# The tiles that TensorE streams begin at other addresses of SBUF; the weights' addresses keep their remainder

## The chip, the cores and the metric

The kernel runs on one core of one Trainium2 chip. The metric is device time in microseconds of one execution, here the median of several. One such execution was also profiled, and all rows below come from it.

SBUF is addressed by partition and by byte within the partition. Each of the 128 partitions holds the same layout, so a tile has one start address, counted in bytes within a partition. This case is about that number, and mostly about its remainder after division by 512.

## The reference

An encoder of two layers on 256 tokens of width 1024, in float32:

```python
for l in range(DEPTH):                      # DEPTH = 2
    x = x + 0.5 * swiglu_ffn(rms_norm(x, norm_w[l, 0]), ffn_w_in[l, 0], ffn_w_out[l, 0])
    h = rms_norm(x, norm_w[l, 1])
    j = l // 2
    if l % 2 == 0:
        x = x + attn_conv_mixer(h, ...)     # differential attention beside a 31-tap convolution
    else:
        x = x + gated_deltanet_mixer(h, ...) # a delta rule in both directions
    x = x + 0.5 * swiglu_ffn(rms_norm(x, norm_w[l, 2]), ffn_w_in[l, 1], ffn_w_out[l, 1])
return rms_norm(x, final_norm_w)

def swiglu_ffn(h, w_in, w_out):             # w_in: 1024 x 5632, w_out: 2816 x 1024
    gate, up = jnp.split(h @ w_in, 2, axis=-1)
    return (jax.nn.silu(gate) * up) @ w_out
```

So there are four feed-forward blocks (FFN 1 to 4), and between them the attention mixer (behind FFN 1) and the delta mixer (behind FFN 3).

## The kernel before, in words

**Matrix products.** x is kept transposed, features on partitions and 256 tokens along the free dimension. Almost every matrix product is made by `column`: one 128 x 128 block of weights is loaded into TensorE and 256 tokens stream past it. Both sides are split into two float32r parts (`hi` and `lo` of the weights, `xh` and `xl` of the normed x, `hh` and `hl` of the hidden layer, `ch` and `cl` of the attention mixer's output, `oo` of the delta mixer's), and each block costs three products:

```python
nc.tensor.matmul(out, hi, xh[:, k, :], start=start and k == ks[0], stop=False)
nc.tensor.matmul(out, hi, xl[:, k, :], start=False, stop=False)
nc.tensor.matmul(out, lo, xh[:, k, :], start=False, stop=stop and k == ks[-1])
```

These are lines 99 to 101 for `xh`, `xl` and for `hh`, `hl` (an FFN's second product), lines 743 to 747 for `ch`, `cl` and lines 1294 to 1296 for `oo`. Every product has a weight load of its own (PEld in the profile), which runs beside the product ahead of it. The tile that is written second in a profile's row (`hi` or `lo` in `acc<-xh,hi`) is the weights, the first one is what streams. A few products go the other way (`rows`, lines 126 to 128): there `xh` and `xl` are the weights, and 512 columns of `hi` or `lo` stream.

**Weights.** `split_next` reads sixteen-block rows of an array half a row (eight blocks, 512 KB) at a time by a DMA of the SP queue into `raw`; ScalarE writes the rounded `hi`, VectorE or GpSimd the rest `lo`. There are up to six sets of these three tiles, three that live through the whole program and three more of most phases.

**Order.** Every engine's order is that of the code, which calls generators of side work (`tick`) between the products. An FFN is 22 calls of `pair` (48 products each) with the gate's work on VectorE, ScalarE and GpSimd behind them, and then eight calls of `column` over the 22 tiles of `hh` (66 products each).

**Addresses.** Pools of tiles lie one behind another in the order in which they are opened, and tiles within a pool of single tiles in the order in which they are made; nothing in the code names an address. The constant pool starts at byte 16512 of a partition, and `normw` (192 bytes), `x` (8192), `ident` (512), `mhalf` (64), `ones` (512), `xh` and `xl` (8192 each) follow. That puts `xh` at 25984 = 50 x 512 + 384. The steps within `xh`, `hh`, `ch` and `oo` are 1024 bytes (one k tile of 256 tokens), and those within `hi` and `lo` 512 bytes (one block), so that all slices of a tile have the remainder of its start.

Of the kernel before, what the change touches and what calls it, by code (L numbers as in the profile page):

```python
# [27 lines left out]

def halves(w, on_pool=()):
    """The weights eight blocks at a time, and whether GpSimd splits them."""  # L30
    n = 2 * w.shape[0]
    return [(w[i // 2, :, i % 2 * 8 : i % 2 * 8 + 8, :], i in on_pool) for i in range(n)]


def plan(g, *srcs):
    """Order in which the weights of a phase are read: (array, split on Pool, parts)."""
    g.plan = [(*s, 1)[:3] for s in srcs]
    g.ready, g.left = [], []


def split_next(g):
    """Read 128 x 128 blocks of weights and split them into two float32r parts."""
# [30 lines left out]
def tick(g):  # L73
    """Advance the work that runs beside the projections."""
    for task in list(g.tasks):
        task[2] += task[1]
        while task[2] >= 1:
            task[2] -= 1
            if next(task[0], g) is g:
                g.tasks.remove(task)  # L80
                break
# [11 lines left out]
def column(g, out, ks, xh, xl, start=True, stop=True):  # L93
    """out[feature, token] += weights^T x over the k tiles of one feature tile."""
# [9 lines left out]
def pair(g, xh, xl):  # L104
    """Two feature tiles of a projection of the width of the model."""
# [7 lines left out]
def rows(g, banks, k0, xh, xl):  # L113
    """banks[t][token, feature] += x^T weights over four k tiles and 512 features."""
# [29 lines left out]
class Norm:  # L144
    """The factor of a root mean square norm, by token as a column and along every row."""
# [7 lines left out]
    def operand(self, f, scale=None):  # L153
        """The two parts of feature tile f of x, weighted."""
# [23 lines left out]
    def rest(self):  # L178
        """Sum over the features, power, and the diagonal matrix that spreads it."""
# [35 lines left out]
def close(g, st, f, acc, scale):  # L215
    """x += scale * acc in feature tile f, and what the next norm needs of it."""
# [12 lines left out]
def ffn(g, wi, wo, st, wcol, aside=iter(())):  # L229
    nc, tc = g.nc, g.tc  # L230
    with tc.tile_pool(name="ffn", bufs=1) as fp, tc.tile_pool(name="ffn2", bufs=2) as f2:
        hh = fp.tile([P, KF, T], F32R, name="hh")
# [43 lines left out]
def start(ctx, tc, a):  # L276
# [10 lines left out]
    nc.sync.dma_start(g.normw, a["norm_w"])  # L287
    g.x = g.const.tile([P, KD, T], F32, name="x")
    g.ident = g.const.tile([P, P], F32, name="ident")
    g.mhalf = g.const.tile([P, 16], F32, name="mhalf")  # L290
    nc.gpsimd.memset(g.mhalf, -0.5)
    g.ones = g.const.tile([P, P], F32, name="ones")
    nc.gpsimd.memset(g.ones, 1.0)
    g.xh = g.const.tile([P, KD, T], F32R, name="xh")
    g.xl = g.const.tile([P, KD, T], F32R, name="xl")
# [22 lines left out]
def first_pair(g, src, pool):  # L318
    """The first two feature tiles, k tile by k tile as x and the weights arrive."""
# [32 lines left out]
def finish(g, a, st):  # L352
    """The last norm: its factor spread over the rows, times the weighted x."""
# [12 lines left out]
def weight_pools(g, es, n):  # L366
    """Room for n more tiles of weights."""
# [3 lines left out]
def phase(g, es, n, **psum):  # L371
    """Weight buffers and PSUM banks of one phase."""
# [12 lines left out]
def ac_consts(g, a, c):  # L385
    """Constants of the mixer, a step at a time: loads, products, and the table of biases."""
# [47 lines left out]
def conv_pair(g, c, n, uT, y, others):  # L434
    """Taps n and up of the depthwise convolution for two channel tiles, one step at a time."""
# [23 lines left out]
def conv_pool(g, ap, c, n, uT, y):  # L459
    """The first n taps with products on ScalarE and sums on GpSimd."""  # L460
# [21 lines left out]
def head(g, ap, h, qT, kz, v, ch, cl, held=False):  # L482
    """One head of the attention in four steps."""
# [84 lines left out]
def staggered(gens):  # L568
    """Each generator starts one slot after the one before it."""
# [10 lines left out]
def conv_norm(g, ap, y, room, ch, cl):  # L580
    """Layer norm over the channels and silu; room holds as much as y."""
# [31 lines left out]
def attn_conv(g, a, st, wcol):  # L613
    nc, tc = g.nc, g.tc
    win, wo = a["ac_in"], a["ac_out"]
    with tc.tile_pool(name="acm", bufs=1) as mp, tc.tile_pool(name="ac2", bufs=g.nt) as ap:
        ch = mp.tile([P, 16, T], F32R, name="ch")
        cl = mp.tile([P, 16, T], F32R, name="cl")
        uT = mp.tile([P, KD, T + 2 * HC], F32, name="uT")
        y = mp.tile([P, KD, T], F32, name="y")  # L620
# [16 lines left out]
        def conv_all():  # L637
            """Up to two pairs of channel tiles side by side."""
# [58 lines left out]
        def scores_done():  # L697
            """The products of the first four heads have been issued."""
# [105 lines left out]
def gates(g, a, c, both, st, beta, gg):  # L804
    """beta and the log decay g, [token, tile, direction and head]."""
# [44 lines left out]
def short_conv(g, acc, dst, w0, ready, sums=None):  # L850
    """Five taps over tokens of two channel tiles, then silu; dst is [channel, 2, token].

    sums takes the sums of squares over the channels and eps, [token, tile, head]."""
# [33 lines left out]
def base_inverse(g, pk, Lp, d):  # L887
    """Inverse of I + L for the 16-blocks of the diagonal, one per partition; [k, i] and [i, k]."""
# [5 lines left out]
    for s in range(1, BB):  # L894
# [4 lines left out]
        tmp = pk.tile([n, BB - 1, BB - 1], F32, tag=f"tmp{d}", name="tmp")  # L899
# [10 lines left out]
def together(*its):  # L910
    """Step by step through several generators side by side."""
# [8 lines left out]
def pace(it, n):  # L920
    """n steps of a generator for each of this one."""
# [10 lines left out]
def delta_net(g, a, st, wcol):  # L932
    nc, tc = g.nc, g.tc
    win = a["gd_in"]
    with ExitStack() as es:
# [4 lines left out]
        tp = ent(tc.tile_pool(name="gdt", bufs=1))  # L940
        big = ent(tc.tile_pool(name="gbig", bufs=9))
# [30 lines left out]
        def square(t):  # L972
            """Sixteen matrices in DRAM, [row, matrix, column]."""
            return bass.AP(t.tensor, t.offset, [[P, P], [PITCH, 16], [1, P]])

        def diagonal(t):
            """The 16-blocks on their diagonals, [matrix and block, row, column]."""
# [10 lines left out]
        def decays():  # L988
            """exp of the sums of g between two tokens, zero on the masked side; kept in qk."""
# [27 lines left out]
        def kgrams(hg):  # L1017
            """L transposed: k k^T with its decays and weights."""
# [479 lines left out]
```

## Time and profile before

| | us |
|---|---|
| median of 3 runs | 1267.43 |
| lowest and highest run | 1266.06, 1270.07 |
| span of the profiled execution, first to last instruction | 1266.3 |

The three runs' times include what lies around the span; the profiled execution has no time of its own beside its span, and lies 1.1 us below the median. TensorE's clock was granted at 0.974 of full speed on the mean.

How the profile is read: PE is TensorE's products and PEld its weight loads, which run beside them; DVE is VectorE, ACT ScalarE, POOL GpSimd. A product's row has a start that is measured and an end that is modelled; products overlap, so 280 ns of one product do not mean that 280 ns pass between two. What passes between two is the distance of their starts, here called the spacing. Where a row of a tile's view gives the first and the last start of n products of one line, and every third product is of that line, the spacing is the difference of the two divided by 3 (n - 1).

### The profile page before, as it was taken

The numbers are of one execution on the slowest core, as the hardware profiler recorded it, in microseconds if no ns is written. First come the engines' busy times: TensorE is split into PE (matmuls) and PEld (weight loads), VectorE is DVE, ScalarE is ACT, GpSimd is POOL, SyncE is SP. The second block draws the span as 40 slices with busy tenths as digits, with TensorE's granted clock in tenths as the row PEclk, the third lists the DMA queues.
The fourth block names the chain that finished last, engine by engine and source line by source line (L and its number), as shares of the span: only waits on it lengthen the run. The fifth ranks groups of instructions, "written<-read, shape, count | busy, mean of one in ns | idle before, by whom it ended". The sixth has DMA issues, their size and how long they took to land.

```text
span 1266.3 us, 23706 instructions
## 1 busy us (share of the span) xinstructions
PE 1199.8 (95%) x9592; PEld 1164.4 (92%) x9592; DVE 800.1 (63%) x1250; ACT 631.2 (50%) x976; POOL 376.5 (30%) x322
## 2 busy tenths in 40 slices
PE   7999999997899999999999999999889987999997
PEld 7999999986679999999999999889869977999996
DVE  7665663999965766655565655577964555665541
ACT  6444445658876644444444444564433334444441
POOL 1111018979913311101311101147620035211101
PEclk9999999998989999999999999999889997999998
DMA  9855656454314555555565554446460025655540
GB/s 309 267 186 185 192 192 191 158 183 148 113 42 149 167 187 187 187 188 184 178 188 187 185 184 143 142 143 189 133 193 2 1 72 162 197 186 184 188 145 34
DMA packets 75325, 204.17 MB, mean 161 GB/s; under 512 B 15912, under 2 KB 26792, under 8 KB 75088
## 3 DMA queue, kind: packets, MB, share of 16 engines
q1 hardware_dynamic: 74208, 201.93, 49.7%
q8 instruction: 75, 1.23, 0.4%
q10 hardware_dynamic: 1008, 0.74, 0.2%
q14 instruction: 34, 0.28, 0.1%
HBM read 197.12 MB, written 7.62 MB: 162 GB/s over the span
## 4 chain that ended last, share of the span: by engine, by line
PE 56%; DVE 5%; DMA 2%; ACT 1%; issue 1%; POOL 0%; SPq 0%; DVEq 0%; ACTq 0%; POOLq 0%
PE acc L99 16%; PE acc L101 16%; PE acc L100 15%; PE acc L985 6%; DVE tmp L900 1%; DVE lo L56 1%; ACT hi L55 1%; DMA raw<-in_gd_out_dram 1%; DMA raw<-in_wi_dram 1%; DVE r L862 1%; PE tr L1151 1%; DVE kq L862 1%; PE tr L1006 0%; DMA raw<-in_gd_in_dram 0%; DMA lp<-gl 0%
## 5 line engine op out<-in xcount | busy, mean ns | idle before, releaser
L55 ACT CAST hi<-raw 128x1024 fp32r<-128x1024 f32 (+1 forms) x360 | 374.6, 1043 | 478.0 <-PE acc L100 296.1
L56 DVE TENSOR_TENSOR lo<-raw,hi 128x1024 fp32r<-128x1024 f32 (+1 forms) x305 | 387.2, 1272 | 248.5 <-ACT hi L55 244.4
L99 PE MATMUL acc<-xh,hi 128*128 128x256 f32 x1840 | 518.7, 283 | 7.9 <-DVE x L218 5.0
L101 PE MATMUL acc<-xh,lo 128*128 128x256 f32 x1840 | 516.5, 281 | 2.3 <-DVE lo L56 2.3
L100 PE MATMUL acc<-xl,hi 128*128 128x256 f32 x1840 | 517.4, 281 | 0.9 <-DVE xl L161 0.9
L99 PEld LDWEIGHTS acc<-xh,hi 128*128 128x128 f32 x1840 | 347.8, 189 | 11.5 <-issue 8.3
L101 PEld LDWEIGHTS acc<-xh,lo 128*128 128x128 f32 x1840 | 348.2, 189 | 3.2 <-DVE lo L56 2.9
L100 PEld LDWEIGHTS acc<-xl,hi 128*128 128x128 f32 x1840 | 347.7, 189 | 2.3 <-DVE xl L161 1.3
L101 PE MATMUL acc<-hh,lo 128*128 128x256 f32 x704 | 197.3, 280 | 0.0
L99 PE MATMUL acc<-hh,hi 128*128 128x256 f32 x704 | 197.3, 280 | 0.0
L100 PE MATMUL acc<-hl,hi 128*128 128x256 f32 x704 | 197.3, 280 | 0.0
L251 POOL TENSOR_TENSOR s<-s,bc 128x512 f32<-128x512 f32 x44 | 78.4, 1783 | 372.4 <-ACT s L250 372.4
L56 POOL TENSOR_TENSOR lo<-raw,hi 128x1024 fp32r<-128x1024 f32 x55 | 132.2, 2411 | 73.0 <-ACT hi L55 72.7
L99 PEld LDWEIGHTS acc<-hh,hi 128*128 128x128 f32 x704 | 133.7, 190 | 0.0
L101 PEld LDWEIGHTS acc<-hh,lo 128*128 128x128 f32 x704 | 133.7, 190 | 0.0
L100 PEld LDWEIGHTS acc<-hl,hi 128*128 128x128 f32 x704 | 133.7, 190 | 0.0
L176 POOL TENSOR_TENSOR sum<-sum,sq 128x256 f32<-128x256 f32 x41 | 40.3, 983 | 216.7 <-ACT sq L172 216.1
L478 POOL TENSOR_TENSOR y<-y,tp 128x256 f32<-128x256 f32 x80 | 70.7, 910 | 9.8 <-ACT tp L475 9.5
L447 DVE SCALAR_TENSOR_TENSOR cv<-uT,convw,cv 128x256 f32<-128x256 f32 x154 | 66.3, 481 | 0.6
L242 DVE TENSOR_TENSOR h<-acc,s 128x512 f32<-128x512 f32 x44 | 30.4, 691 | 27.6 <-PE acc L101 24.2
L249 DVE TENSOR_TENSOR s<-acc,bc 128x512 f32<-128x512 f32 x44 | 30.2, 691 | 23.0 <-PE acc L101 22.6
L161 DVE SCALAR_TENSOR_TENSOR xl<-x,normw,xh 128x256 fp32r<-128x256 f32 x48 | 36.5, 778 | 12.7 <-ACT xh L160 12.7
(260 smaller groups left out, 1413.1 us busy)
## 6 DMA issues: line engine op xcount, KB each, us to landing
raw<-in_wi_dram SPq DMA_DIRECT2D x172, 512.0 KB, 4.5
raw<-in_wo_dram SPq DMA_DIRECT2D x88, 512.0 KB, 4.4
raw<-in_ac_in_dram SPq DMA_DIRECT2D x40, 512.0 KB, 4.4
raw<-in_gd_in_dram SPq DMA_DIRECT2D x32, 512.0 KB, 3.9
raw<-in_ac_out_dram SPq DMA_DIRECT2D x16, 512.0 KB, 3.8
raw<-in_gd_out_dram SPq DMA_DIRECT2D x8, 512.0 KB, 5.4
raw<-in_wi_dram SPq DMA_DIRECT2D x8, 256.0 KB, 5.1
scr<-row SPq DMA_DIRECT2D x1, 2048.0 KB, 10.6
```

Of the source, the lines that this page charges most:

```text
L55: nc.scalar.copy(hi[sl], raw[sl])
L56: eng.tensor_tensor(lo[sl], raw[sl], hi[sl].bitcast(F32), op=ALU.subtract)
L99: nc.tensor.matmul(out, hi, xh[:, k, :], start=start and k == ks[0], stop=False)
L100: nc.tensor.matmul(out, hi, xl[:, k, :], start=False, stop=False)
L101: nc.tensor.matmul(out, lo, xh[:, k, :], start=False, stop=stop and k == ks[-1])
L161: nc.vector.scalar_tensor_tensor(g.xl[:, f, :], x[:, f, :], w, g.xh[:, f, :].bitcast(F32), op0=ALU.mult, op1=ALU.subtract,)
L176: nc.gpsimd.tensor_tensor(self.sum, self.sum, sq, op=ALU.add)
L242: nc.vector.tensor_tensor(h, acc, s, op=ALU.mult)
L251: nc.gpsimd.tensor_tensor(s, s, over(st.bc), op=ALU.mult)
L447: nc.vector.scalar_tensor_tensor(y[:, ct, :] if j == CW - 1 and not n else cv[:, i, :], uT[:, ct, j : j + T], g.convw[:, ct, j : j + 1], c ...
L478: nc.gpsimd.tensor_tensor(y[:, ct, :], y[:, ct, :], tp, op=ALU.add)
L985: nc.tensor.matmul(ps[:, h, :], lhsT(h), rhs(h), start=True, stop=True)
```

## The change: what it does

The edits are unused tiles that move what comes behind them (`skip`), another order of five constants, and one tile made larger (`tmp`, from 15 x 15 to 16 x 16 values). No instruction is added or removed, and on every engine the instructions stand in the order in which they stood, but for the two memsets of `ones` and `mhalf` on GpSimd at the very start, which trade places. The start addresses become these (remainder after division by 512; counts are products in the program):

| streamed tile | products | before | after |
|---|---|---|---|
| `xh`, `xl` (FFN, mixers) | 5520 | 384 | 0 |
| `hh`, `hl` of FFN 1 | 528 | 256 | 256 |
| `hh`, `hl` of FFN 2 and 3 | 1056 | 64 | 256 |
| `hh`, `hl` of FFN 4 | 528 | 96 | 256 |
| `ch`, `cl` | 384 | 256 | 256 |
| `oo` | 192 | 416 | 256 |
| `hi`, `lo` in `rows` (512 columns) | 192 | 64 | 64 |
| float32 tiles of the delta mixer (`r2`, `F0`, `F1`, `kq`) | some 600 | 96, 416 | 256 |
| `ident`, `kz`, `y`, `v0`, `v1`, `ones` | some 300 | 192 to 384 | 0 or 256 |

The weights `hi` and `lo` have remainder 64 before and after. Where the tiles of the lower rows are themselves loaded as weights (`xh` in `rows`, `r2`, `F0`, `qT`, `both`), that remainder changes with them.

```diff
+def skip(pool, n, name):
+    if n:
+        pool.tile([P, n // 4], F32, name=name)
...
-def ffn(g, wi, wo, st, wcol, aside=iter(())):
+def ffn(g, wi, wo, st, wcol, skipped, aside=iter(())):
     nc, tc = g.nc, g.tc
     with tc.tile_pool(name="ffn", bufs=1) as fp, tc.tile_pool(name="ffn2", bufs=2) as f2:
+        skip(fp, skipped, "skip_h")
         hh = fp.tile([P, KF, T], F32R, name="hh")
...
     nc.sync.dma_start(g.normw, a["norm_w"])
+    skip(g.const, 192, "skip_x")
     g.x = g.const.tile([P, KD, T], F32, name="x")
+    g.xh = g.const.tile([P, KD, T], F32R, name="xh")
+    g.xl = g.const.tile([P, KD, T], F32R, name="xl")
     g.ident = g.const.tile([P, P], F32, name="ident")
+    g.ones = g.const.tile([P, P], F32, name="ones")
+    nc.gpsimd.memset(g.ones, 1.0)
     g.mhalf = g.const.tile([P, 16], F32, name="mhalf")
     nc.gpsimd.memset(g.mhalf, -0.5)
-    g.ones = g.const.tile([P, P], F32, name="ones")
-    nc.gpsimd.memset(g.ones, 1.0)
-    g.xh = g.const.tile([P, KD, T], F32R, name="xh")
-    g.xl = g.const.tile([P, KD, T], F32R, name="xl")
+    skip(ent(tc.tile_pool(name="skip", bufs=1)), 320, "skip_w")
     g.kept_weights = weight_pools(g, ctx, 3)
...
+        skip(mp, 64, "skip_y")
         y = mp.tile([P, KD, T], F32, name="y")
...
-        tmp = pk.tile([n, BB - 1, BB - 1], F32, tag=f"tmp{d}", name="tmp")
+        tmp = pk.tile([n, BB, BB], F32, tag=f"tmp{d}", name="tmp")
...
+        skip(tp, 160, "skip_b")
         big = ent(tc.tile_pool(name="gbig", bufs=9))
...
-        st = ffn(g, a["wi"][1], a["wo"][1], st, 3)
-        st = ffn(g, a["wi"][2], a["wo"][2], st, 4)
+        st = ffn(g, a["wi"][1], a["wo"][1], st, 3, 192)
+        st = ffn(g, a["wi"][2], a["wo"][2], st, 4, 192)
...
-        st = ffn(g, a["wi"][3], a["wo"][3], st, None)
+        st = ffn(g, a["wi"][3], a["wo"][3], st, None, 160)
```

## Rows read from the trace of the kernel before

**Rows 1.** The page: busy time by engine; clock granted to TensorE in 40 slices.

```profile
PE 1199.8 (95%) x9592; PEld 1164.4 (92%) x9592; DVE 800.1 (63%) x1250; ACT 631.2 (50%) x976; POOL 376.5 (30%) x322
...
PEclk9999999998989999999999999999889997999998
```

**Rows 2.** Groups by line: shapes, count | busy us, mean ns | idle before.

```profile
L101 PE MATMUL acc<-xh,lo 128*128 128x256 f32 x1840 | 516.5, 281 | 2.3 <-DVE lo L56 2.3
...
L126 PE MATMUL acc<-hi,xh 128*128 128x512 f32 x64 | 25.2, 407 | 0.6 <-DVE x L218 0.6
...
L985 PE MATMUL acc<-r,Lt 128*128 128x128 f32 x192 | 24.2, 284 | 0.0
```

**Rows 3.** Windows: stretch, length, busy (instructions) by engine, clock, DMA share, GB/s.

```profile
core 0: us, PE busy (x) PEld busy (x) DVE busy (x) ACT busy (x) POOL busy (x), PEclk, DMA share, GB/s
30.00:137.00 107.00, 107.00 (x911) 107.00 (x910) 66.58 (x69) 50.51 (x59) 19.41 (x11) 1.00 0.65 214
137.00:197.00 60.00, 60.00 (x531) 60.00 (x531) 35.16 (x37) 28.89 (x37) 7.11 (x7) 1.00 0.60 192
440.00:547.00 107.00, 107.00 (x910) 107.00 (x910) 66.12 (x68) 51.54 (x60) 18.86 (x11) 1.00 0.58 191
547.00:611.00 64.00, 64.00 (x536) 64.00 (x535) 34.12 (x37) 29.05 (x38) 10.31 (x8) 1.00 0.56 181
625.00:736.00 111.00, 111.00 (x944) 111.00 (x944) 69.19 (x70) 52.09 (x61) 20.04 (x11) 1.00 0.60 189
816.00:922.00 106.00, 97.77 (x747) 92.41 (x746) 85.50 (x227) 56.52 (x87) 56.21 (x29) 0.95 0.53 157
1081.00:1193.00 112.00, 112.00 (x953) 112.00 (x952) 70.36 (x71) 52.33 (x61) 20.05 (x11) 1.00 0.59 189
```

**Rows 4.** Tile hl in FFN 1 to 4: count, ns min/median/max, first and last start.

```profile
L100 PE MATMUL acc<-hl,hi x176: 276/276/279, 137.2 to 196.7; 128*128 128x256 f32 x176
...
L100 PE MATMUL acc<-hl,hi x175: 283/283/283, 547.7 to 610.4; 128*128 128x256 f32 x175
...
L100 PE MATMUL acc<-hl,hi x175: 282/283/283, 736.4 to 799.0; 128*128 128x256 f32 x175
...
L100 PE MATMUL acc<-hl,hi x175: 277/278/281, 1193.7 to 1254.6; 128*128 128x256 f32 x175
```

**Rows 5.** Tile xl, the same view, in FFN 1 and FFN 4.

```profile
L100 PE MATMUL acc<-xl,hi x255: 280/280/280, 40.0 to 129.8; 128*128 128x256 f32 x128
...
L100 PE MATMUL acc<-xl,hi x315: 279/279/279, 1081.7 to 1192.6; 128*128 128x256 f32 x158
```

**Rows 6.** Tile cl, the same view, two stretches of the attention mixer's output product.

```profile
L746 PE MATMUL acc<-cl,hi x10: 281/281/281, 404.2 to 410.2; 128*128 128x256 f32 x10
...
L746 PE MATMUL acc<-cl,hi x15: 276/276/332, 412.6 to 417.2; 128*128 128x256 f32 x15
```

**Rows 7.** Tile xl at the end of the attention mixer; tile oo in the delta mixer.

```profile
L100 PE MATMUL acc<-xl,hi x10: 276/276/281, 316.8 to 319.8; 128*128 128x256 f32 x10
...
L1295 PE MATMUL acc<-oo,hi x18: 278/283/343, 1047.1 to 1053.0; 128*128 128x256 f32 x18
```

**Rows 8.** Timeline of PE where FFN 1's second product begins: start us, length us, product.

```profile
136.94 0.28 PE L101 MATMUL acc<-xh,lo 128*128 128x256 f32 x1
137.05 0.28 PE L99 MATMUL acc<-hh,hi 128*128 128x256 f32 x1
137.17 0.28 PE L100 MATMUL acc<-hl,hi 128*128 128x256 f32 x1
137.29 0.28 PE L101 MATMUL acc<-hh,lo 128*128 128x256 f32 x1
137.40 0.28 PE L99 MATMUL acc<-hh,hi 128*128 128x256 f32 x1
137.51 0.28 PE L100 MATMUL acc<-hl,hi 128*128 128x256 f32 x1
```

**Rows 9.** Line 245 on VectorE (writes hl) in FFN 1 and FFN 2; line 900.

```profile
L245 DVE TENSOR_TENSOR hl<-h,hh x8: 683/684/686, 49.0 to 128.1; 128x512 fp32r<-128x512 f32 x8
...
L245 DVE TENSOR_TENSOR hl<-h,hh x8: 684/684/686, 459.2 to 538.3; 128x512 fp32r<-128x512 f32 x8
...
L900 DVE TENSOR_TENSOR tmp<-tt,lp x30: 157/306/2181, 884.0 to 920.5; 128x1 f32<-128x1 f32 x2, 128x4 f32<-128x4 f32 x2, 128x9 f32<-128x9 f32 x2, 128x16 f32<-128x16 f32 x2
```

More of the change, by code (lines that the diff above doesn't have):

```diff
@@ L368, in weight_pools, with phase @@
     return [es.enter_context(g.tc.tile_pool(name=m, bufs=n)) for m in WEIGHTS]
-def phase(g, es, n, **psum):
+def phase(g, es, n, skipped, **psum):
+    if skipped:
+        skip(es.enter_context(g.tc.tile_pool(name="skip", bufs=1)), skipped, "skip_w")
     g.weights = [g.kept_weights] + ([weight_pools(g, es, n)] if n else [])
@@ L616, in attn_conv @@
     with tc.tile_pool(name="acm", bufs=1) as mp, tc.tile_pool(name="ac2", bufs=g.nt) as ap:
+        skip(mp, 0, "skip_c")
         ch = mp.tile([P, 16, T], F32R, name="ch")
@@ L1365, in encoder @@
     with ExitStack() as es:
-        phase(g, es, 3, acc=3, tr=2, cv=2, sc=1)
+        phase(g, es, 3, 0, acc=3, tr=2, cv=2, sc=1)
         with tc.tile_pool(name="acc_", bufs=1) as c:
@@ L1369, in encoder @@
                 g.first, st = fp, first_norm(g, 0, fp)
-                st = ffn(g, a["wi"][0], a["wo"][0], st, 1, ac_consts(g, a, c))
+                st = ffn(g, a["wi"][0], a["wo"][0], st, 1, 0, ac_consts(g, a, c))
             g.pool_in, g.pool_out, g.conv_off = range(4, 28), (), 0
             st = attn_conv(g, a, st, 2)
-        st = ffn(g, a["wi"][1], a["wo"][1], st, 3)
-        st = ffn(g, a["wi"][2], a["wo"][2], st, 4)
+        st = ffn(g, a["wi"][1], a["wo"][1], st, 3, 192)
+        st = ffn(g, a["wi"][2], a["wo"][2], st, 4, 192)
     g.post_rate, g.gram_rate, g.dec_rate, g.nr2, g.order = 3, 4, 2, 11, "kqvz"
@@ L1377, in encoder @@
     with ExitStack() as es:
-        phase(g, es, 0, acc=5, tr=3)
+        phase(g, es, 0, 0, acc=5, tr=3)
         st = delta_net(g, a, st, 5)
     with ExitStack() as es:
-        phase(g, es, 3, acc=4, tr=2)
+        phase(g, es, 3, 0, acc=4, tr=2)
         final_weight(g, a, es.enter_context(tc.tile_pool(name="fin", bufs=1)))
-        st = ffn(g, a["wi"][3], a["wo"][3], st, None)
+        st = ffn(g, a["wi"][3], a["wo"][3], st, None, 160)
         finish(g, a, st)
```

## The prediction

> **What bounds the kernel now.** I read the page first: TensorE is busy 95% of the span and its clock is granted in full nearly everywhere [rows 1]. The windows by stage say where that is more than an average: in the long stretches of the four FFNs PE is busy for all of 107, 111 or 112 us, while VectorE is busy for some 62% and ScalarE for 47% [rows 3], and no wait is counted there. In these stretches the time is the number of products times the distance between two starts. So I looked for that spacing by operand, with the tile view of a third of the products at a time.
>
> The reader is to see four numbers. The first FFN's second product runs from 137.2 to 196.7 us with 176 products of `hl`: 59.5 us / (3 x 175) = 113.3 ns. The same code on the same weight buffers in FFN 2 takes 62.7 / (3 x 174) = 120.1 ns, in FFN 3 62.6 / 522 = 119.9, in FFN 4 60.9 / 522 = 116.7 [rows 4]. `xl` takes 89.8 / 762 = 117.8 ns in FFN 1 and 110.9 / 942 = 117.7 in FFN 4 [rows 5]. The modelled length of a product follows its spacing (276, 283 and 279 ns), so a length can stand for the spacing where too few starts are there.
>
> What differs between FFN 1 and FFN 2 is the start of `hh` and `hl`: remainder 256 against 64 modulo 512. FFN 1 runs faster with no less beside it (192 GB/s against 181, VectorE 35 us against 34 of a similar stretch) [rows 3]. And the spacing changes where the operand does: coming from `xh` at 384, the starts of FFN 1's first `hh` products lie 120, 120, 110 and 110 ns apart in the two printed places [rows 8]. So the address matters, by up to 6%: 256 gives 113.3 ns, 96 gives 116.7, 384 gives 117.8, 64 gives 120.0.
>
> It is not the whole story. `ch` and `cl` already stand at 256, and in the attention mixer's output product they run at either of two paces, 281 ns long in one stretch and 276 in the next [rows 6]. I sorted the sixteen stretches of eight or more products there: nine settle at 276, seven at 281, and a stretch keeps its pace from its first few products to its end. `xl` at 384 was once at 276 too, just behind a stretch at half clock [rows 7]. I read this as two stable patterns of product and weight load, of which a start address makes one likelier; each interruption chooses anew.
>
> **The change, part by part.**
>
> *`xh` and `xl` from 384 to 0.* This is the big term, and 0 itself is not in the trace. The bounds are the best and the worst row, 113.3 and 120.0 ns. I take 0 to act as 256, because among the four measured remainders the only multiple of 256 is also the one fast residue; that is an inference from one residue. At the fast pattern the gain is 117.8 - 113.3 = 4.5 ns per product. The four long stretches hold 911 + 910 + 944 + 953 = 3718 of these products [rows 3]: 16.7 us. The remaining 5520 - 3718 = 1802 stand at the FFNs' starts and in the mixers, where PE also waits, or runs at half clock: from 816 to 922 us it is busy 97.8 of 106 us at a granted 0.95 with VectorE at 85.5 [rows 3]. I count half: 900 x 4.5 = 4.0 us.
>
> *`hh` and `hl`.* FFN 2 and 3: 1056 x (120.0 - 113.3) = 7.1 us. FFN 4: 528 x (116.7 - 113.3) = 1.8 us. FFN 1 stays at 256. All are wholly bound by PE.
>
> *`oo` from 416 to 256.* 192 products, 283 ns long on the median against 276 [rows 7]: 6.5 ns, half of them beside waits: 0.6 us.
>
> With the fast pattern everywhere the sum is 16.7 + 4.0 + 7.1 + 1.8 + 0.6 = 30.2 us. With the slow one of 256 (281 ns, about 117.8) everywhere, `xh` gains nothing, FFN 2 and 3 gain 2.3, FFN 4 loses 0.6 and FFN 1 loses 528 x 4.5 = 2.4: a loss of 0.7 us. The stretches of the attention mixer say nine to seven; the long FFN stretches begin behind short float32 products, as most of the fast ones there did, so I take 0.65 for the fast one: 0.65 x 30.2 - 0.35 x 0.7 = 19.4 us.
>
> *Nothing, with their bounds.* Float32 products of the delta mixer (some 670 of 128 columns, as L985 [rows 2]) go from 96 and 416 to 256 in both operands; a row of theirs at 256 does not exist, and the same spread of 6% on 112 ns gives 4.5 us either way where PE alone bounds, which it does not there. `rows` has `xh` as weights at 0 instead of 384: 192 products, at 6% of some 233 ns 2.7 us either way. VectorE, ScalarE and GpSimd don't seem to feel an address: line 245 takes 684 ns writing `hl` at 256 and at 64 [rows 9]. `tmp` with rows of 16 values instead of 15 touches thirty products on VectorE between 884 and 921 us, of 306 ns each on the median [rows 9]; 5% of their 18.5 us would be 0.9 us. All of these at nothing. The unused tiles cost space only: the buffers and their number stay, and so does the weights' 64.
>
> *What is late next.* At 113.3 ns eight blocks of weights last 24 x 113.3 = 2.7 us, 193 GB/s; FFN 1's second product already drew 192 and the FFN's first 214 [rows 3]. VectorE at 66.6 us of 107 becomes 65% of 103. Nothing else takes the bound in the FFNs.
>
> The profiled span of 1266.3 us less 19.4 is 1246.9; the runs' median lies 1.1 us above that span, so **1248 us**.
>
> [...] The trace has 113.3 and 120.0 ns for products that differ in the streamed operand's address alone [rows 4]. [...]
>
> **The rivals.**
>
> *B. 0 is no 256.* The unit is 512 bytes, `xh` at 0 stays at its 117.8, and only `hh` and `oo` gain: 7.1 + 1.8 + 0.6 = 9.5 us, 1258. For it: of the residues measured only 256 itself is fast. FFN 1 shows that `hh` at 256 falls into the fast pattern from `xh` at the slow one [rows 8], so this gain would hold.
>
> *C. No effect.* The FFNs differ by something else than the address, or the stretches all settle on the slow pattern of 256: 1267 to 1268. For it: the seven slow stretches of `cl` [rows 6]. Against it: FFN 2 and FFN 3 agree to 0.2 ns over 522 products each [rows 4].
>
> *D. Slower.* `xh` at 0 collides with the weights at 64, as `hh` at 64 does. At 120.0 ns the long stretches lose 3718 x 2.2 = 8.2 us and the others 900 x 2.2 = 2.0; `hh` and `oo` give 9.5 back, so 1268. It decides against the change by more than a measurement's 0.3% (3.8 us) from 4618 x d > 13.3, d = 2.9 ns or 120.7 ns, beyond the worst mean of the rows; at 124 ns (as far above 120 as 113.3 to 117.8) the time is 1267.4 + 4618 x 6.2 / 1000 - 9.5 = 1287. For it: two residues that are both 64 are the slowest pair measured. Against it: 0 and 64 differ.
>
> **How the numbers follow.** 0.3% is about what a measurement here can tell from no change. Forecast A (0 as 256, patterns mixed) 0.62, from 1237 (all fast) to 1262 (a quarter of the gain); B 0.14; C 0.10, of which the rule of two ports, taken alone, 0.04; D 0.14, a third of it within 0.3%. The top of A, nearly all stretches slow, is within 0.3% too and has 0.02 of its 0.62; a fast pattern below 113.3 ns, or float32 products that gain as well, would go below 1235 and has a few hundredths. Faster: A and B less the top of A, 0.74. Same: C, that top and a third of D, 0.16. Slower: the rest of D, 0.10. The range of 1235 to 1270 leaves out the far end of D and the lowest corner of A. A's own range is 1237 to 1262.
>
> **What would show it.** In the profile after: `hl` in FFN 2, 3 and 4 at lengths of 276 and spacings of 113 ns, as in FFN 1; `xl` in the four long stretches at 276 or 281, one value for a whole stretch, with spans from the first to the last start of some 3 x 113.3 ns per product where it is 276; VectorE's and ScalarE's times unchanged. B shows `xl` at 279 in every stretch; D at 283 or more; C leaves `hl` in FFN 2 at 281 or 283. I am wrong in the mechanism if `hl` in FFN 2 and 3 keeps 283 at its new address, and in the size if the spacing falls but PE then waits inside the FFNs.

## The result, and the profile after

| | median, us | lowest to highest | runs |
|---|---|---|---|
| kernel before, same chip | 1268.75 | 1266.06 to 1271.28 | 4 |
| changed kernel | 1248.39 | 1245.03 to 1249.78 | 4 |

The ratio of the times is 0.9852, with a 95% interval of 0.9820 to 0.9883: 20 us, or 1.5%, faster. The profiled execution of the changed kernel was the fastest of its four, 1245.03 us, with a span of 1243.2; that of before has a span of 1266.3, so the two traces differ by 23.1 us, 3 more than the medians.

The page: busy time by engine, and TensorE's granted clock in 40 slices. It answers to [rows 1].

```profile
PE 1178.8 (95%) x9592; PEld 1145.0 (92%) x9592; DVE 799.9 (64%) x1250; ACT 632.3 (51%) x976; POOL 377.2 (30%) x322
...
PEclk9999999998999999999999999999889997999998
```

TensorE does the same 9592 products in 21.0 us less; the other engines' times stay. Next the groups by line that answer to [rows 2] and to line 900 (now 913).

```profile
L107 PE MATMUL acc<-xh,lo 128*128 128x256 f32 x1840 | 515.7, 281 | 2.4 <-DVE lo L62 2.4
...
L132 PE MATMUL acc<-hi,xh 128*128 128x512 f32 x64 | 25.1, 404 | 0.6 <-DVE x L224 0.6
...
L999 PE MATMUL acc<-r,Lt 128*128 128x128 f32 x192 | 24.7, 288 | 0.0
...
L913 DVE TENSOR_TENSOR tmp<-tt,lp 128x1 f32<-128x1 f32 (+14 forms) x30 | 18.0, 626 | 2.1 <-DMA lp<-gl 2.1
```

The mean length of the main product is 281 ns, as before. One who stops there finds no effect. The stages tell more. The windows, which answer to [rows 3]:

```profile
core 0: us, PE busy (x) PEld busy (x) DVE busy (x) ACT busy (x) POOL busy (x), PEclk, DMA share, GB/s
30.00:133.00 103.00, 103.00 (x910) 103.00 (x910) 66.77 (x69) 51.03 (x59) 19.29 (x11) 1.00 0.68 222
133.30:193.10 59.80, 59.80 (x530) 59.80 (x529) 35.16 (x37) 28.90 (x37) 6.98 (x7) 1.00 0.60 194
430.00:537.00 107.00, 107.00 (x909) 107.00 (x910) 66.19 (x68) 51.68 (x60) 18.74 (x11) 1.00 0.58 191
537.40:599.60 62.20, 62.20 (x531) 62.20 (x530) 33.89 (x36) 28.81 (x37) 10.32 (x8) 1.00 0.57 183
614.00:725.00 111.00, 111.00 (x945) 111.00 (x944) 69.14 (x70) 52.08 (x62) 19.95 (x11) 1.00 0.59 189
...
1060.00:1171.00 111.00, 111.00 (x982) 111.00 (x981) 72.52 (x74) 54.75 (x64) 20.63 (x12) 1.00 0.60 197
```

FFN 1 issues 910 products in 103 us where it took 107, FFN 4 issues 982 in 111 us where it issued 953 in 112. FFN 2 and FFN 3 have the pace of before: 909 in 107 us, 945 in 111. The tiles say the same, `hl` in FFN 1 to 4 first (they answer to [rows 4]), then `xl` in the long stretches of FFN 1 to 4 ([rows 5] has two of them).

```profile
L106 PE MATMUL acc<-hl,hi x176: 276/276/276, 133.4 to 192.9; 128*128 128x256 f32 x176
...
L106 PE MATMUL acc<-hl,hi x176: 281/281/281, 537.5 to 599.3; 128*128 128x256 f32 x176
...
L106 PE MATMUL acc<-hl,hi x176: 281/281/281, 724.9 to 786.8; 128*128 128x256 f32 x176
...
L106 PE MATMUL acc<-hl,hi x176: 276/276/276, 1172.0 to 1231.5; 128*128 128x256 f32 x176
...
L106 PE MATMUL acc<-xl,hi x304: 276/276/281, 30.0 to 133.1; 128*128 128x256 f32 x152
...
L106 PE MATMUL acc<-xl,hi x304: 281/281/281, 430.1 to 537.1; 128*128 128x256 f32 x152
...
L106 PE MATMUL acc<-xl,hi x314: 281/281/281, 614.0 to 724.6; 128*128 128x256 f32 x157
...
L106 PE MATMUL acc<-xl,hi x329: 276/276/279, 1059.7 to 1171.6; 128*128 128x256 f32 x165
```

In these stretches there are two lengths, and one for a whole stretch: in FFN 1 and 4 276 ns, spacing 59.5 us / 525 = 113.3 ns; in FFN 2 and 3 281 ns, 61.8 / 525 = 117.7 and 61.9 / 525 = 117.9. (281 and the 279 ns that `xl` had before both go with 117.8 ns: a length is a hint, the starts are the measure.)

**Where the 23.1 us come from.** Cut at the first start of each stage, the FFNs give: FFN 1 3.8 us in its first product and 0.0 in its second; FFN 2 0.2 and 1.2; FFN 3 0.0 and 1.1; FFN 4 4.6, and 1.7 with the end: 12.6 us. The mixers give 10.5: attention 0.9 up to its output product and 5.1 in that, delta 1.9 and 2.6. (How long PE waits at the start of FFN 1 differs from one execution to the next: in the six profiled executions, here and below, in which its `xh` is fast, its first product ends between 132.6 and 137.5 us. So its 3.8 us are those of this execution; by the spacing 888 products are worth 4.0.) The large piece is in the windows of the attention mixer's output product (336.6 to 419.0 us before, 331.9 to 409.3 after). The kernel before: the whole part, its first 7 us, the 13.5 us behind them, and the last stretch at half clock.

```profile
336.60:419.00 82.40, 75.11 (x508) 66.32 (x507) 54.31 (x136) 58.68 (x148) 27.17 (x51) 0.90 0.33 105
...
337.00:344.00 7.00, 4.03 (x25) 2.96 (x23) 6.92 (x17) 6.26 (x20) 6.73 (x10) 1.00 0.53 167
344.10:357.60 13.50, 11.04 (x32) 7.66 (x33) 8.50 (x26) 6.22 (x22) 6.00 (x14) 0.50 0.15 49
...
378.30:381.50 3.20, 3.20 (x11) 2.12 (x11) 2.49 (x9) 3.20 (x8) 0.00 (x0) 0.50 0.66 219
```

The changed kernel: the whole part, the stretch ahead of its one fall of the clock, and that fall.

```profile
331.90:409.30 77.40, 70.60 (x509) 62.71 (x508) 54.56 (x136) 59.05 (x149) 27.50 (x51) 0.98 0.34 112
...
325.00:333.70 8.70, 5.86 (x25) 3.88 (x23) 8.70 (x18) 8.37 (x18) 8.45 (x12) 1.00 0.36 115
333.90:337.10 3.20, 3.08 (x8) 2.07 (x9) 3.12 (x5) 2.84 (x10) 3.05 (x5) 0.50 0.65 218
```

The whole part in three experiments below: in `e4_x256`, whose FFNs run as those of the changed kernel, then in `e8_kick_d` and `e7_kick_c`, which have its addresses throughout:

```profile
331.90:414.10 82.20, 74.02 (x496) 64.99 (x497) 54.37 (x138) 58.75 (x149) 27.31 (x53) 0.90 0.33 105
...
336.70:418.90 82.20, 74.94 (x508) 66.08 (x507) 54.36 (x136) 58.81 (x149) 27.27 (x51) 0.90 0.33 105
...
334.20:412.90 78.70, 71.47 (x509) 64.03 (x508) 54.52 (x136) 59.19 (x149) 27.57 (x51) 0.96 0.34 111
```

In both kernels the granted clock falls from 1.00 to 0.50, the only two levels in the two traces: before at 344.1 us, behind a stretch in which PE is busy for 4.0 us of 7.0, after at 333.9, behind one in which it is busy for 5.9 of 8.7. Before, it stayed there for 13.5 us and once more for 3.2; after, for 3.2 in all. That is 13.5 us less at half clock, worth up to 6.8 us (an estimate from the granted 0.50, as if the clock alone set the time there), and the part is 5.0 us shorter. `e4_x256` and `e8_kick_d` have the clock of before (0.90) and its length (82.2 us) with the streamed operands and weights of this part where the change put them; at 0.96 the part lasts 78.7 us in `e7_kick_c` and 78.9 in `e3_hh`, where `xh` stands as before. So these 5 us go with the clock that an execution was granted, not with the addresses. The rest of the gain does not: over all measured executions with a mean clock of 0.979 to 0.982, 12 of before have a median of 1264.9 us and 3 of the changed kernel lie between 1245.0 and 1247.8, some 19 us apart.

### The profile page after: what moved, and what is told of

It is laid out like the page before. It is cut to its first block, busy times and chain, and to the rows that moved or that the text cites. A ratio compares the mean times of both kernels' runs of the same rounds, so it can differ in the third digit from the quotient of the medians.

```text
span 1243.2 us, 23706 instructions
## 1 busy us (share of the span) xinstructions
PE 1178.8 (95%) x9592; PEld 1145.0 (92%) x9592; DVE 799.9 (64%) x1250; ACT 632.3 (51%) x976; POOL 377.2 (30%) x322
## 4 chain that ended last, share of the span: by engine, by line
PE 57%; DVE 5%; DMA 1%; ACT 1%; issue 1%; POOL 0%; SPq 0%; DVEq 0%; ACTq 0%; POOLq 0%
PE acc L105 16%; PE acc L106 16%; PE acc L107 16%; PE acc L999 6%; DVE tmp L913 1%; DVE lo L62 1%; ACT hi L61 1%; DMA raw<-in_gd_out_dram 1%; PE acc L1308 1%; PE acc L1309 1%; DVE r L875 1%; PE acc L1310 1%; PE tr L1165 1%; DVE kq L875 1%; PE tr L1020 0%
## 5 line engine op out<-in xcount | busy, mean ns | idle before, releaser
L106 PE MATMUL acc<-xl,hi 128*128 128x256 f32 x1840 | 516.3, 281 | 1.0 <-DVE xl L167 1.0
L106 PEld LDWEIGHTS acc<-xl,hi 128*128 128x128 f32 x1840 | 348.4, 189 | 2.6 <-DVE xl L167 1.4
L106 PE MATMUL acc<-hl,hi 128*128 128x256 f32 x704 | 196.1, 278 | 0.0
L106 PEld LDWEIGHTS acc<-hl,hi 128*128 128x128 f32 x704 | 132.1, 188 | 0.0
```

## The experiments

Below, the difference is the start of the streamed operand less that of the weights, modulo 256. Before it is 64 for `xh`, 192 for `hh` in FFN 1, 0 in FFN 2 and 3, 32 in FFN 4; in the changed kernel 192 for all of these. A to D are the prediction's forecast and its rivals. A stretch is called fast where its products start 113.3 ns apart, and slow where it is 117.8.

**The changed kernel once more (`e1_again`).** Only a comment is added.

> The changed kernel unchanged, executed and profiled once more. If each interruption chooses the pattern by chance, the four FFNs show another mix of 276 and 281 ns than fast, slow, slow, fast, and the time moves by 3.5 to 6 us for each FFN that differs. If the place in the program fixes the pattern, FFN 1 and 4 are at 276 and FFN 2 and 3 at 281 again, within 2 us of 1245.

1245.85 us (1 run), span 1244.0. FFN 1 and 4 are fast and FFN 2 and 3 slow again; `xl` in FFN 1 and FFN 2:

```profile
L106 PE MATMUL acc<-xl,hi x300: 276/276/276, 30.1 to 131.7; 128*128 128x256 f32 x150
...
L106 PE MATMUL acc<-xl,hi x303: 281/281/281, 430.2 to 536.9; 128*128 128x256 f32 x152
```

In the attention mixer the mean spacing of the `xh` products moved, from 116.6 to 113.9 ns (of the spacings under 140 ns). So in these two executions the pattern of a long FFN stretch comes with its place in the program, that of short stretches between interruptions does not. For FFN 2 even that does not hold further on: `e7_kick_c` and `e9_two` are the same program up to FFN 2's third pair, and in both its long `xh` stretch is fast already ahead of that pair.

**A map of the addresses (`e2_map`).** The encoder is left out. 90 pairs of remainders, each with five stretches of 24 products, between float32 products (in the trace those of the first two pairs ran ahead, and their five stretches are one):

```
for w in (0, 32, 64, 128, 192, 256, 320, 384, 448):
    for m in (0, 64, 96, 128, 160, 192, 256, 320, 384, 448):
        out = ps.tile([P, T], F32, tag="acc", name=f"m{m}w{w}e")
        for r in range(5):
            between(r % 3)
            products(out, m, w)
```

> Leaves the encoder out: it only makes products of 256 columns in the kernel's order of three, for ten remainders of the streamed tile and nine of the weights, five stretches of 24 products each behind a short float32 product. Theory that the difference of the two addresses decides: streamed 64 on weights 64 (120.0 ns) is as streamed 0 on 0, 128 on 128, 256 on 256, 320 on 320. Theory that the streamed address alone decides, by its remainder modulo 256: every row of weights shows 113.3 or 117.8 ns at 0 and 256, 120.0 at 64 and 320. Theory that 512 is the unit: 0 and 256 differ on the weights at 64.

Tiles are named by streamed remainder (m) and weights' remainder (w). Lengths of 276, 281 and 283 ns go with spacings of 113.3, 117.8 and 120.0.

```profile
L1402 PE MATMUL m0w0e<-xl,hi x40: 283/283/283, 11.4 to 37.4; 128*128 128x256 f32 x40
...
L1402 PE MATMUL m0w64e<-xl,hi x40: 276/276/281, 339.1 to 354.0; 128*128 128x256 f32 x40
...
L1402 PE MATMUL m64w64e<-xl,hi x40: 280/283/283, 354.6 to 370.2; 128*128 128x256 f32 x40
...
L1402 PE MATMUL m64w128e<-xl,hi x40: 276/276/283, 514.7 to 529.8; 128*128 128x256 f32 x40
...
L1402 PE MATMUL m192w0e<-xl,hi x40: 276/276/282, 99.9 to 115.0; 128*128 128x256 f32 x40
```

Streamed 0 is slowest with weights at 0 and has the fast pattern with weights at 64. Streamed 64 is slowest with weights at 64 and has it with 128. All 442 stretches that the trace shows, sorted by the difference, from the starts (means over the last fifteen starts of a stretch):

| difference | pairs | stretches | spacing, ns |
|---|---|---|---|
| 0 | 16 | 76 | 119.8 to 120.0 |
| 32 | 6 | 30 | 116.4 to 117.9 |
| 64 | 17 | 81 | 117.7 to 117.9 |
| 96 | 6 | 30 | 119.8 to 120.1 |
| 128 | 17 | 85 | 63 at 118.4 to 118.9, 22 at 120.0 |
| 160 | 6 | 30 | 10 at 117.3 to 117.5, 20 at 118.4 to 118.9 |
| 192 | 16 | 80 | 42 at 113.3 to 113.4, 38 at 117.7 to 117.9 |
| 224 | 6 | 30 | 118.1 to 118.7 |

The period is 256 bytes, and neither address counts alone: of 72 comparisons of two pairs that differ by 256 in one of the addresses, with five stretches each, 350 of 360 stretches had the same spacing in both, to 0.6 ns. That also suggests that the choice of a pattern repeats where the products ahead are alike. C (no effect) is refuted, and B (0 does not act as 256) too. Differences of 128 and 160 hold two paces as well, which the expectation of `e6_kick` below overlooks; but in the map only 192 reaches 113.3 ns.

**`hh` alone (`e3_hh`).** The kernel before, with `hh` at 256 in FFN 2 to 4; `xh` stays at 384.

```
+        if skipped:
+            fp.tile([P, skipped // 4], F32, name="skip_h")
...
+        st = ffn(g, a["wi"][1], a["wo"][1], st, 3, 192)
+        st = ffn(g, a["wi"][2], a["wo"][2], st, 4, 192)
...
+        st = ffn(g, a["wi"][3], a["wo"][3], st, None, 160)
```

> The kernel before with the streamed hidden layer alone moved to 256; x stays at 384. If a stretch that comes from 384 always falls into the fast pattern, as FFN 1's did, hl is at 276 ns in all four FFNs and the time 7.1 + 1.8 = 8.9 us lower, 1259. If the pattern is chosen anew with even chances, one or two of FFN 2 to 4 are at 281 and the time is 1261 to 1265. If the hidden layer's address does nothing, 1268.

1265.6 us (10 runs), ratio 0.9999 [0.9973, 1.0025]: no change. The profiled execution is the fastest of the ten, 1259.28 us. `hl` in FFN 2 and 4, and `xl` in FFN 2:

```profile
L100 PE MATMUL acc<-hl,hi x163: 281/281/281, 544.8 to 602.0; 128*128 128x256 f32 x163
...
L100 PE MATMUL acc<-hl,hi x176: 281/281/281, 1183.9 to 1245.7; 128*128 128x256 f32 x176
...
L100 PE MATMUL acc<-xl,hi x295: 276/276/276, 439.9 to 539.9; 128*128 128x256 f32 x148
```

`hh` fell into the slow pattern in FFN 2, 3 and 4, one more than the second branch had allowed. By the spacings that gives 2 x 528 x (120.0 - 117.8) = 2.3 us in FFN 2 and 3 and costs 528 x (117.8 - 116.7) = 0.6 in FFN 4: 1.7 us, which this measurement can't tell from nothing. (`xh`, still at 384, was not to gain.) Also, FFN 2's `xh`, at difference 64, ran a whole stretch at 276 ns (100.0 us / 882 = 113.4): that difference has a fast pattern too, though none of the map's 81 stretches there found it. It took FFN 2's first product from 128.3 to 124.0 us in this execution, without any change to `xh`.

**256 in place of 0 (`e4_x256`).** The changed kernel with `xh`, `xl` and the constants behind them at 256.

```
-    skip(g.const, 192, "skip_x")
+    skip(g.const, 448, "skip_x")
...
-    skip(ent(tc.tile_pool(name="skip", bufs=1)), 320, "skip_w")
+    skip(ent(tc.tile_pool(name="skip", bufs=1)), 64, "skip_w")
```

> The changed kernel with x's two parts at 256 instead of 0 (the float32 constants behind them move to 256 too), weights at 64 as before. If 256 bytes are the unit, xl again is at 276 or 281 ns in whole stretches and the time is 1238 to 1258, about 1248. If 512 are the unit, xl shows a third length, or one pattern alone: 1238 with 276 everywhere, 1258 with 281 everywhere.

1253.35 us (6 runs), ratio 0.9892 [0.9858, 0.9927], within the range expected and not clear of the changed kernel's 0.9852; FFN 1 and 4 fast, FFN 2 and 3 slow, as with 0. Its span of 1250.7 us is 7.5 over the changed kernel's, of which 4.8 lie in the attention mixer's output product, in the window shown above.

**The weights moved too (`e5_w0`).** The changed kernel with the weights at 0 modulo 512: now streamed operands and weights all begin at multiples of 256.

```
-    skip(ent(tc.tile_pool(name="skip", bufs=1)), 320, "skip_w")
+    skip(ent(tc.tile_pool(name="skip", bufs=1)), 256, "skip_w")
...
-        st = ffn(g, a["wi"][1], a["wo"][1], st, 3, 192)
+        st = ffn(g, a["wi"][1], a["wo"][1], st, 3, 256)
```

and so in the other places, so that `hh`, `ch` and the delta mixer's tiles keep their addresses.

> The changed kernel with its weights moved from 64 to 0 modulo 512, so that every streamed operand and every weight begins at a multiple of 256 bytes. The output is the reference's. Theory 1, it is the difference of the two addresses modulo 256 that sets the spacing: streamed minus weights is 0 now, so every xh stretch and every hh stretch runs at 120.0 ns with no second pattern; the hh part of the second FFN goes back from 62.2 us to about 63.4, of the first FFN from 59.8 to 63.4, the whole comes out at 1266 to 1280 us, not faster than before by the measurement, and 18 to 30 us over the changed kernel. Theory 2, the streamed address alone decides (a multiple of 256 is good): as the changed kernel, 1248 us, spacings of 113.3 and 117.8 ns.

1282.34 us (4 runs), ratio 1.0122 [1.0084, 1.0160]: 15 us slower than before, with every streamed operand where the change put it. `hl` in FFN 1 and 2:

```profile
L106 PE MATMUL acc<-hl,hi x176: 283/283/283, 142.3 to 205.3; 128*128 128x256 f32 x176
...
L106 PE MATMUL acc<-hl,hi x176: 283/283/283, 556.0 to 619.0; 128*128 128x256 f32 x176
```

63.0 us / 525 = 120.0 ns, in all four FFNs, and PE is busy for 1216.8 us instead of 1178.8. The difference decides, in the whole kernel as in the map; a streamed address at a multiple of 256 is worth nothing by itself. The time came out 2 us above the range expected, and 34 over the changed kernel where I had put 30 at most.

**What sets the pattern (`e6_kick`).** The encoder is left out. Difference 192; 12 products, one short interruption, 24 products, nine times for each of twenty interruptions, behind three kinds of float32 products in turn.

> The encoder is left out; the output is not the reference's. Streamed operand at 256, weights at 64 modulo 512 (difference 192, the only one with two patterns). Stretches of 24 products, each after 12 products of its own kind and one of twenty kinds of short interruption, nine times each: none, one product of 16 to 512 columns, one 256-column product at another streamed remainder, several such, one or two float32 products. Theory 1, the pattern is set by what stands at the interruption: some kind of interruption sends nine of nine into 113.4 ns, whatever the stretch ran at before, and with none the pattern of the 12 products goes on. Theory 2, it is chance: every kind gives a mix, and about half of the stretches run at 113.4.

In the trace the engine's order differs from the program's text in some kinds. Where nothing was to interrupt, the float32 products ran ahead too, and all that is left is one stretch of some 420 products, at 113.3 ns to its end. The kinds of two and four products, and the shortest float32 one, lie spread among the products of the stretches. For the others the answer depends on the kind: a product of 16 columns left nine of nine at 117.8, three of which had been fast; one float32 product of 256 columns turned each of nine round, fast to slow and slow to fast (and where there were two, of 64 columns, the second stood five or six products behind the first, and every stretch ended at the pace that it had ahead of both). A product of 192 columns kept two fast stretches fast and turned five of seven slow ones fast, and so did a 256-column product whose streamed operand was at difference 128. The tile before and behind such a 192-column product:

```profile
L1402 PE MATMUL pre_col_d<-xl,hi x4: 278/281/281, 197.6 to 198.7; 128*128 128x256 f32 x4
...
L1402 PE MATMUL out_col_d<-xl,hi x8: 276/276/281, 199.2 to 201.6; 128*128 128x256 f32 x8
```

No kind that stood in its place sent nine of nine into the fast pattern, as theory 1 wanted; but neither is it a coin, since the same interruption behind the same products mostly gave the same answer: the two slow stretches that the 192-column product left slow are those behind the first kind of float32 product, the five that it turned are those behind the other two.

**The same in the kernel (`e7_kick_c`, `e8_kick_d`).** The changed kernel with such a product ahead of 12 columns in FFN 2 and in FFN 3; `e8_kick_d` has the other kind in the same places.

```
         hi, lo = block(g)
+        if g.kick and k == ks[0]:
+            nc.tensor.matmul(out[:, 0:192], hi, xh[:, 0, 0:192], start=True, stop=True)
...
+            g.kick = skipped == 192 and j in (2, 3, 4)
```

> The changed kernel with one product of 192 columns put ahead of each of the 12 columns of the third to fifth pairs of gate and up in the second and the third FFN (24 products in all; each writes where the next product starts anew, so the output is the reference's). Theory 1, a short interruption of this kind moves a stretch from the slow pattern to the fast one and leaves a fast one fast, as it did in the run of single kicks: from about the third pair on the second and third FFN run at 113.3 ns, each gains some 1,300 products at 4.45 ns, 5.8 us, less 12 times some 110 ns for the kicks, so 4 to 5 us each and 8 to 10 us in all: 1238 to 1241 us. Theory 2, the pattern falls by chance or is fixed by what came before the stretch: spacings stay 117.8 ns, and the kicks cost 2.6 us: 1251 us.

> The same with another kick: one product of 256 columns whose streamed operand begins at 192 modulo 512, so that its difference to the weights is 128. Theory 1: as the other kick, 113.3 ns from about the third pair of the second and third FFN on, 1238 to 1242 us. Theory 2: spacings stay at 117.8 ns, 1251 us.

1240.02 us (4 runs), ratio 0.9783 [0.9738, 0.9828], and 1245.86 us (4 runs), 0.9801 [0.9747, 0.9856]. In both traces FFN 2 and 3 run at 276 ns behind the first of these products. First `xl` of FFN 3 in `e7_kick_c`, up to the first of them (at 621.3 us, with two of the 29 behind it) and behind the last; then `xl` of FFN 2 in `e8_kick_d`, ahead of the first (at 445.2) and behind the last:

```profile
L108 PE MATMUL acc<-xl,hi x29: 277/281/283, 611.9 to 621.9; 128*128 128x256 f32 x29
...
L108 PE MATMUL acc<-xl,hi x197: 276/276/276, 653.0 to 719.7; 128*128 128x256 f32 x197
...
L108 PE MATMUL acc<-xl,hi x14: 281/281/281, 440.1 to 444.7; 128*128 128x256 f32 x14
...
L108 PE MATMUL acc<-xl,hi x198: 276/276/278, 476.9 to 543.9; 128*128 128x256 f32 x198
```

`e8_kick_d` misses its expected time by 4 us with the spacings as expected. Its profiled execution has a mean clock of 0.973 and a span of 1243.6 us, against 0.981 and 1234.4 in `e7_kick_c`: of the 9.2 us, 3.4 lie in the attention mixer's output product (82.1 us at a clock of 0.90, 78.7 at 0.96) and 2.5 in FFN 1's first product, where PE waits longer at the start and is at half clock for 3.4 us.

**Four products in place of 24 (`e9_two`).** The 192-column product only ahead of the third gate pair's two columns.

```
+            g.kick = skipped == 192 and j == 2
             acc = first_pair(g, wi[0], g.first) if g.first else pair(g, g.xh, g.xl)
+            g.kick = False
```

> The changed kernel with the 192-column product only ahead of the two columns of the third gate pair of the second and the third FFN, four products in all. If one such product is enough to move a stretch to the fast pattern and nothing moves it back, all four FFNs run at 113.3 ns for the rest as with twelve, and the kernel gains on the one with twelve the 20 products left out at some 110 ns, 2 us: 1235 to 1239 us. If it needs several, one of the two FFNs stays at 117.8 ns: 1241 to 1245 us.

1238.84 us (6 runs; before on the same chip 1264.82 in 11), ratio 0.9786 [0.9753, 0.9820]: the fastest version here by the median, 26 us under before; it is not clear of `e7_kick_c`, whose interval holds its ratio. FFN 2 and 3 together take 184.2 + 182.1 = 366.3 us, where the changed kernel takes 190.3 + 188.2 = 378.5. The timeline of PE in FFN 3: start us, length us, product.

```profile
619.96 0.28 PE L107 MATMUL acc<-xh,hi 128*128 128x256 f32 x1
620.07 0.28 PE L108 MATMUL acc<-xl,hi 128*128 128x256 f32 x1
620.19 0.28 PE L109 MATMUL acc<-xh,lo 128*128 128x256 f32 x1
620.31 0.25 PE L106 MATMUL acc<-xh,hi 128*128 128x192 f32 x1
620.40 0.30 PE L107 MATMUL acc<-xh,hi 128*128 128x256 f32 x1
...
621.01 0.28 PE L109 MATMUL acc<-xh,lo 128*128 128x256 f32 x1
621.12 0.28 PE L107 MATMUL acc<-xh,hi 128*128 128x256 f32 x1
621.23 0.28 PE L108 MATMUL acc<-xl,hi 128*128 128x256 f32 x1
621.35 0.28 PE L109 MATMUL acc<-xh,lo 128*128 128x256 f32 x1
```

L106 is the added product. Ahead of it starts are 0.11 to 0.12 us apart, 117.8 ns on the mean of eighteen; six products behind it they are 0.34 us for three, 113.3 ns each; the stretch stays so, over the second added product and to the end of FFN 3's second product. Its tile `hl` over all four FFNs:

```profile
L108 PE MATMUL acc<-hl,hi x704: 276/276/276, 135.9 to 1226.3; 128*128 128x256 f32 x176
```

In both traces with the 192-column product FFN 2 was fast before its first added product already, so a turn is seen in FFN 3 of both and in FFN 2 and 3 of `e8_kick_d`: four of four. Without an added product none of the six slow stretches of FFN 2 and 3 turned, in the changed kernel, `e1_again` and `e4_x256`. What FFN 2 gains in `e7_kick_c` and `e9_two` is therefore not shown to come from the added products; what it does in the executions without a trace is not known.

## Why the prediction was right, point by point

The forecast of 1248 us stands beside 1248.39. The mechanism, a spacing that an address sets and two patterns of it, was right as far as it went; that the sum fits to 0.4 us is luck in part, since the terms miss in both directions.

- **What bounds it.** Right. The FFNs' long stretches fell by the spacing times the products and by nothing else, and PE waits for nothing in their long stretches, as before.
- **"I take 0 to act as 256."** Right in effect (`e4_x256`: same patterns), for an incomplete reason. What I read off one residue as a property of the streamed address is one of the difference to the weights: at 64 modulo 512 the weights make 0 and 256 a difference of 192, the only one in the map with the fast pattern. `e5_w0` moves the weights alone and turns the gain into a loss.
- **"Two stable patterns", each interruption choosing anew.** Right as to the two: 113.3 and 117.8 ns, nothing else in the FFNs' long stretches. The choice is less free than I took it to be: the FFNs' mix was the same in all three profiled executions at difference 192 without an added product, FFN 1 and 4 were fast in all six with and without one, and one product of 192 columns could change a stretch. Only FFN 2 differs, fast by itself in two of six. Nor does `hh` choose by itself: it begins right behind `xh`, not behind float32 products as the reason for the 0.65 has it, and in all 24 FFNs of these six traces it kept the pace of its `xh`.
- **`xh` in the long stretches, 16.7 us at 0.65 fast: 10.9.** Two of four stretches were fast, FFN 1 and 4. In the stages that hold them it is 3.8 + 0.2 + 0.0 + 4.6 = 8.6 us, the FFNs' starts included. Too large by the share taken for fast, right in the gain of a fast stretch.
- **`hh`, 8.9 us if fast everywhere, with the 0.65 applied 0.65 x 8.9 - 0.35 x 0.7 = 5.5.** FFN 4 fast, FFN 2 and 3 slow: 1.2 + 1.1 + 1.7 = 4.0.
- **The other `xh` products and `oo`, 4.6 x 0.65 = 3.0 us.** The mixers gave 10.5 in the profiled execution. Of these 5 are the attention mixer's output product, where the clock was 0.98 instead of 0.90, a term that the prediction didn't have. It hides that the FFNs gave 12.6 where some 16 were forecast: the sum is better than its terms. Without the clock's 5 the two traces differ by 18 us, and the mixers by 5.5 instead of 3.0; their single stages vary by that much from one execution to the next (the delta mixer ahead of its output product is 1.9 us shorter than before here and 1.0 longer in `e8_kick_d`). The clock's share can't be counted as a gain of the change: `e1_again` has it again, `e4_x256` and `e8_kick_d` don't.
- **Nothing for the rest.** Right: by the starts, `rows` went from a median of 233 ns to 229, some 0.8 us in all, and the delta mixer's products of `r` and `Lt` stayed at 112 ns (their lengths, 404 against 407 and 288 against 284 [rows 2], are no measure); `tmp` took 18.0 us against 18.5.
- **Rival B**, and in it the step that FFN 1's fall from a slow `xh` into the fast pattern [rows 8] "would hold" elsewhere. Refuted: in `e3_hh` the `hh` of FFN 3 and 4 came from a slow `xh`, as FFN 1's had, and settled slow; FFN 2's came from a fast one and settled slow too.
- **Rival C.** Refuted by the map: 113.3 to 120.0 ns by the two addresses alone. The rule of two ports, 0.04 of this rival's 0.10, is shown by no run; in its place the runs show a spacing that follows the difference of the two addresses, 119.8 to 120.0 ns at 0 and as low as 113.3 at 192 (`e2_map`), and 120.0 in the kernel with the weights moved to 0 (`e5_w0`). What causes it is in no trace.
- **Rival D.** The slow pair exists, 119.8 to 120.0 ns in all 76 stretches at a difference of 0 (`e2_map`), only not here. "Two residues that are both 64 are the slowest pair" was the truth in a sentence, and "0 and 64 differ" the reason why the change wasn't hit; I had used it as a rival and not seen that it is also the explanation of the gain.

Open: what shifts the clock in the mixers from one execution to the next; why a given interruption leads to a given pattern; why a difference of 192 is the fast one. Not tested: whether an added product would also move the kernel before, whose `xh` at difference 64 was once fast in FFN 2 (`e3_hh`).

## What to carry to other kernels

Where each product loads its own weights and PE is never idle (here 256 columns and 128 x 128 weights in float32r; nothing else was measured), compare the start of the streamed operand with that of its weights modulo 256, not with a round number: here a difference of 192 allowed 113.3 ns and a difference of 0 cost 120.0, 6% of the main loop. Then read the spacing of the starts stretch by stretch, since one kernel can hold two paces, and at a difference of 192 a single extra product moved a stretch that had settled on the slower one (117.8 ns ahead of it, 113.3 behind it, in FFN 3 of `e9_two`). Before a gain is put down to an edit, read the granted clock of each stage in both traces: here 5 of 23 us went with the clock, granted at 0.98 instead of 0.90 in one part.

## What the runs showed of the hardware that I had not expected

- The spacing of a 128 x 256 product with its own weight load follows the difference of two addresses with a period of 256 bytes, from 113.3 to 120.1 ns over eight differences (`e2_map`); moving the weights alone took the kernel from 1248 to 1282 us (`e5_w0`).
- At a difference of 192 two patterns are stable for as long as nothing interrupts (over 1400 products in FFN 2 of the changed kernel, at 117.8 ns). One added product (of 192 columns, or of 256 at another difference) moved each of the four slow stretches that met one in the kernel to 113.3 ns; within six products in the one shown. One of 16 columns left nine of nine short stretches at 117.8, and one float32 product of 256 columns turned nine of nine round (`e6_kick`).
- One stage, the attention mixer's output product, lasted 77.4, 78.7 and 82.2 us in executions with the same addresses of its operands, at a granted clock of 0.98, 0.96 and 0.90.
